# Fourth weight block of the gate/up pairs: residue 64 of 256 bytes in every second pair

## The chip, the core and the metric

The kernel runs on one core of a Trainium2 chip. Its engines work side by side and wait for each other through semaphores: TensorE (PE in the profile, with its weight loads shown apart as PEld), VectorE (DVE), ScalarE (ACT), GpSimd (POOL) and SyncE (SP, which here only issues DMAs). The on-chip memory has 128 partitions; an address below is a byte offset within a partition, the same in all 128. A *residue* is such an address modulo 256. The metric is the device time of one execution in microseconds; a run of a kernel is summed up by the median of its executions.

## The reference

One decoder layer, batch 1, 512 positions, width 1024, all in float32: three token mixers (a gated MLP, a sparse attention and a linear recurrence) side by side, their gated sum through an output projection, and then the feed-forward part, in which the change lies:

```python
hf = rms_norm(x, g_pre_ffn)
f_gate, f_up = jnp.split(hf @ w_ffn_in, 2, axis=-1)
f = (jax.nn.silu(f_gate) * f_up) @ w_ffn_out
return x + rms_norm(f, g_post_ffn)
```

`w_ffn_in` has 2 x 2816 columns: 22 blocks of 128 gate columns and 22 of 128 up columns.

## The kernel before

Every float32 product is made of three products in the type float32r: each operand is split into a high part (ScalarE copies it with rounding, line 125) and a low part (VectorE subtracts, line 130), and TensorE adds high x high, high x low and low x high. Of a matmul's two operands one is *stationary*: 128 x 128, loaded into the array by a weight load of its own. The other is *moving*: 128 partitions by 256 or 512 columns, streamed through. The weight load of one matmul goes on while the matmul ahead of it runs.

The program runs through its stages in one fixed order, written out in the calls at the end of `hybrid_block`: normalisation and the first projections, the recurrent mixer, the gated MLP, the attention, the three gated branches, the output projection (`wo_pass`, line 1059), the gate/up products of the feed-forward part, and its output product (`down`). The order of the work on each engine is that in which the code records it; buffers come from pools in which each tag has a fixed number of buffers, taken in turn.

**The gate/up pairs.** Each of the 22 pairs j is one gate block and one up block. The first two (`HEAD = 2`) are plain products (`ffn_head`). The other 20 are made by `pairs` (line 1315) with Strassen's scheme in Winograd's form: the weights of a pair are cut into four blocks a11, a12, a21, a22 of 128 x 512, the activations in the same way, and seven products replace eight. `pair_prep(j)` (line 1272) makes the weight side of the seven, in steps that are interleaved with the products of pair j - 1: raw weights come by DMA to a tile `rawp`; sums of blocks are formed on VectorE; each block and sum is split into a high and a low tile. The split blocks lie in a ring of five pairs of tiles (`hi`/`lo` and `u`), apart from the block a22, which has two tiles of its own (line 1295): `a22h` (tag "tg") and `a22l` (tag "q32"), each with two buffers, so that pairs alternate between them.

`product_parts(ps, j, a, b)` (line 1306) runs one of the seven products: four steps k, and in each three matmuls (high weights x high activations, high x low, low x high), 12 in all, with a weight slice of 128 x 128 as the stationary operand and an activation tile of 256 columns as the moving one. The product with a22 is called in `last(j)` (line 1321), after the second product of the next pair, and takes the activation side number 4.

**Where the operands lie.** The function `row` hands out tiles of 512 floats from the pool "mid", in three tags. Before the change every tile of the three tags has residue 0, as do the ring's tiles. The activation sides (tiles `t`, and `fh`/`fl`) are allocated with a first element of `MOVED = 16` floats, so they lie at residue 64. The slices of a weight tile are 512 bytes apart and those of an activation tile 1024 bytes, so the residue is the same for all four k.

**The other users of the two tags.** "tg" holds the gates of the branches (`gate_part`, line 1015, 24 tiles in all), "q32" the queries for the compressed attention (`q_tile`, line 733, 8 tiles; they are stationary operands at line 795), and `down` takes two tiles of each for partial sums (line 1437).

For comparison the prediction also uses `v_pair` (line 762), which runs matmuls of 256 columns with stationary slices of `hh`/`hl` and moving slices of weights, all at residue 0: in steps of 128 floats for the stationary operand over c, and 24 matmuls for each c.

Of the kernel before, what the change touches and what calls it, by code (L numbers as in the profile page):

```python
# [23 lines left out]
F32 = mybir.dt.float32  # L24
F32R = mybir.dt.float32r
# [5 lines left out]
S = 512  # L31
# [20 lines left out]
def hybrid_block(ctx: ExitStack, tc: tile.TileContext, A, out):  # L52
# [5 lines left out]
    mid = ctx.enter_context(tc.tile_pool(name="mid", bufs=1))  # L58
# [35 lines left out]
    def nm(s):  # L94
        cnt[0] += 1
        return f"{s}_{cnt[0]}"
# [6 lines left out]
        return t if len(shape) == 1 else t.rearrange(  # L103
            "p (a b) -> p a b" if len(shape) == 2 else "p (a b c) -> p a b c", **dict(zip("abc", shape)))

    def row(name, dt=F32, tag="row"):
        return mid.tile([128, S], dt, tag=tag, name=nm(name), bufs={"row": 6, "q32": 2, "tg": 2}[tag])

    def bank(tag):
        return psum[1].tile([128, S], F32, tag=tag, name=nm(tag), bufs=psum[2][tag])  # L110
# [13 lines left out]
    def split(src, hi, lo, lo_eng=None):  # L124
        res["hi"] = SC.activation(hi, src, AF.Copy)  # L125
        e = lo_eng or V
        if e is GP:
            GP.tensor_sub(lo, src, f32(hi))
        else:
            res["lo"] = V.tensor_sub(lo, src, f32(hi))  # L130
# [41 lines left out]
    HEAD, LASTV = 2, 2  # L172
# [186 lines left out]

    rmul = const.tile([128, 3, 4], F32, name="rmul")  # L360
    rbs = row("rbs")
    half = const0([128, 3, 8], "half")

    def norm():

        for i in range(2):
            for c in range(2):
                SC.activation(xr[i][:, c, :], xr[i][:, c, :], AF.Square, accum_out=ssx[:, 2 * i + c:2 * i + c + 1])
            q = slice(2 * i, 2 * i + 2)
            rsqrt(rstd[:, q], ssx[:, q], 2, 1.0 / D, EPS)  # L370
            V.tensor_scalar(rmul[:, 0, q], rstd[:, q], GELU_K ** 0.5, None, op0=OP.mult)
            V.tensor_scalar(rmul[:, 1, q], rstd[:, q], GELU_C, None, op0=OP.mult)
            V.tensor_mul(rmul[:, 2, q], rstd[:, q], rstd[:, q])
            yield
        few = softplus()
        for _ in range(19):
            next(few, None)
            yield
        rb = bank("tr")
        with tc.issue_after(res["mm"].ins):  # L380
            spread(rb, rstd)
        SC.activation(rbs, rb, AF.Copy)
        yield
        for k in range(NK):
            t = row("h32")
            V.scalar_tensor_tensor(t, xt[k], vec[:, V_PRE + k:V_PRE + k + 1], rbs, op0=OP.mult, op1=OP.mult)
            split(t, hh[k], hl[k])
            yield
        V.tensor_scalar(half[:, 0], vec[:, V_BX:V_BX + 8], 0.5, None, op0=OP.mult)
        V.tensor_scalar(half[:, 1], vec[:, V_LNG:V_LNG + 8], 0.5, None, op0=OP.mult)  # L390
        V.tensor_scalar(half[:, 2], vec[:, V_LNB:V_LNB + 8], 0.5, None, op0=OP.mult)
# [31 lines left out]
    def gelu2(x, dst, c=None):  # L423


        s = row("gs")
        SC.activation(s, x, AF.Square, scale=GELU_K ** 0.5 if c is None else rmul[:, 0, c:c + 1])
        V.scalar_tensor_tensor(s, s, 1.0, x, op0=OP.add, op1=OP.mult)
        SC.activation(s, s, AF.Tanh, scale=GELU_C if c is None else rmul[:, 1, c:c + 1])
        V.scalar_tensor_tensor(dst, s, 1.0, x, op0=OP.add, op1=OP.mult)  # L430
# [780 lines left out]
    def first_weights():  # L1211

        ff["raw"] = [slab("rawp", tag="w2", shape=(2, 1024))]
        pair_load(HEAD)
        for _ in range(9):
            yield
        w = [tuple(wts.tile([128, 1024], F32R, tag=t, name=nm(t), bufs=3) for t in ("hi", "lo")) for _ in range(3)]
        ff["ring"] = w
        ff["prep"] = pair_prep(HEAD)
        for _ in range(4):  # L1220
            next(ff["prep"])
            yield
# [45 lines left out]
    def pair_load(j):  # L1268
        if HEAD <= j < NFF:
            SY.dma_start(ff["raw"][(j - HEAD) % 2], A["w_fi"][2 * j:2 * j + 2].rearrange("u p n -> p u n"))  # L1270

    def pair_prep(j):

        if j >= NFF:
            return
        raw = ff["raw"][(j - HEAD) % 2]
        r4 = raw.rearrange("p u (h n) -> p (u h) n", h=2)
        a11, a12, a21, a22 = (r4[:, i] for i in range(4))
        g = [ff["ring"][(3 * (j - HEAD) + i) % 5] for i in range(3)]
        w = wa[j] = {}  # L1280

        def halves(u, *names):
            for i, n in enumerate(names):
                w[n] = tuple(t[:, 512 * i:512 * i + 512] for t in u)

        split(raw[:, 0], *g[0])
        halves(g[0], "a11", "a12")
        s13 = stage.tile([128, 1024], F32, tag="raw", name=nm("s13"), bufs=2)
        V.tensor_tensor(s13.rearrange("p (i n) -> p i n", i=2), r4[:, 0:4:3], a21[:, None, :].to_broadcast([128, 2, 512]),
                        op=OP.subtract)  # L1290
        yield
        split(s13, *g[1])
        halves(g[1], "s3", "s1")
        yield
        w["a22"] = row("a22h", F32R, "tg"), row("a22l", F32R, "q32")
        split(a22, *w["a22"])
        V.tensor_add(a21, s13[:, 512:], a11)
        yield
        V.tensor_sub(a22, a12, a21)
        yield  # L1300
        split(raw[:, 1], *g[2])
        halves(g[2], "s2", "s4")
        pair_load(j + 2)
        yield
# [10 lines left out]
    def pairs():  # L1315
# [11 lines left out]

        for j in range(HEAD, NFF):
            prep = pair_prep(j + 1)
            z, y = ff["zy"] if j == HEAD else (bank("mm")[:, :256], bank("mm"))  # L1330
            r1, r3 = row("r1"), row("r3")
# [405 lines left out]
```

## Time and profile before

| | |
|---|---|
| median of three runs | 1112.24 us |
| the three runs | 1112.24, 1109.35, 1112.64 us |
| the profiled execution | 1111.33 us |
| its span, first to last instruction | 1109.6 us |
| granted TensorE clock, mean | 0.998 |
| instructions in the span | 15969 |

A row of a group in the profile reads: line, engine, operation, output <- inputs, partitions x elements, count | busy time in us, mean duration of one in ns | idle time of the engine just ahead, and what ended it. An answer for one line or one tile has count, then the shortest, median and longest duration in ns, then the first and last start. A row of stretches reads: start and end in us, length, and then for each engine the busy time and in brackets the count of the instructions that overlap the stretch, and last the granted clock, the share of the DMA engines and GB/s. Where the row is for one line, it has the columns of TensorE and of its weight loads alone. A row of the timeline reads: start, duration, engine, line, operation, and in square brackets the idle time ahead of it and what ended it. Matmuls overlap: the next one starts while the one ahead still drains, so a duration is a latency, and the distance from start to start is the pace.

### The profile page before, as it was taken

How to read it: one execution, taken by the hardware profiler on the slowest of the kernel's cores; microseconds unless marked ns; L12 is line 12 of the kernel's file. 1: busy time of each engine (PE TensorE's matmuls, PEld its weight loads, DVE VectorE, ACT ScalarE, POOL GpSimd, SP SyncE). 2: the span in 40 equal slices, each digit the busy share in tenths (PEclk: the TensorE clock that was granted, in tenths of full speed). 3: DMA queues.
4: the chain of work that ended last, by engine and by line, in shares of the span. 5: the costliest groups of instructions: out<-in, count | busy, mean ns of one | idle time of the engine just before them, and what ended most of it. 6: DMA issues, size and time to landing. Idle time of an engine off the chain costs nothing.

```text
span 1109.6 us, 15969 instructions
## 1 busy us (share of the span) xinstructions
PE 1100.5 (99%) x6152; PEld 951.7 (86%) x6152; DVE 827.9 (75%) x1453; ACT 626.1 (56%) x1120; POOL 46.4 (4%) x59
## 2 busy tenths in 40 slices
PE   9999999999999999999999999999999999999997
PEld 8888778888888887888888888888999999998886
DVE  6966968263575899998998844557988888879665
ACT  6756674232344676876776733435655655567552
POOL 1000203000000000000000000000000000022200
PEclk9999999999999999999999999999999999999999
DMA  8332325323222211102112163331233322378902
GB/s 311 114 95 76 98 94 192 112 82 106 81 91 77 76 58 38 58 20 77 58 39 67 48 241 101 114 115 38 77 115 115 107 104 95 133 192 216 186 33 95
DMA packets 34652, 115.02 MB, mean 104 GB/s; under 512 B 3408, under 2 KB 3696, under 8 KB 33424
## 3 DMA queue, kind: packets, MB, share of 16 engines
q1 hardware_dynamic: 27200, 93.78, 25.4%
q0 software_dynamic: 5216, 11.18, 5.0%
q10 hardware_dynamic: 2160, 9.04, 2.3%
q8 instruction: 48, 0.79, 0.3%
q14 instruction: 28, 0.23, 0.1%
HBM read 111.89 MB, written 2.10 MB: 103 GB/s over the span
## 4 chain that ended last, share of the span: by engine, by line
PE 93%; DVE 4%; ACT 1%; DMA 0%; issue 0%; DVEq 0%
PE mm L242 39%; PE mm L1310 18%; PE mm L1446 7%; PE mm L545 4%; PE mm L1074 4%; PE o L895 4%; PE sc L857 3%; PE tr L882 3%; PE tr L1446 3%; PE mm L773 2%; PE tr L689 1%; PE mm L1176 1%; DVE lo L130 1%; PE tr L470 1%; PE tr L605 1%; PE tr L795 1%
## 5 line engine op out<-in xcount | busy, mean ns | idle before, releaser
L125 ACT ACTIVATE hi<-raw 128x1024 fp32r<-128x1024 f32 (+1 forms) x108 | 113.4, 1050 | 155.4 <-PE mm L242 81.2
L242 PE MATMUL mm<-hh,hi 128*128 128x512 f32 x504 | 199.7, 396 | 0.0
L242 PE MATMUL mm<-hh,lo 128*128 128x512 f32 x504 | 197.5, 392 | 0.2 <-DVE lo L130 0.2
L242 PE MATMUL mm<-hl,hi 128*128 128x512 f32 x504 | 197.1, 391 | 0.0
L130 DVE TENSOR_TENSOR lo<-raw,hi 128x1024 fp32r<-128x1024 f32 (+1 forms) x108 | 132.0, 1222 | 79.3 <-ACT hi L125 72.1
L242 PEld LDWEIGHTS mm<-hh,lo 128*128 128x128 f32 x504 | 94.6, 188 | 19.9 <-DVE lo L130 0.5
L242 PEld LDWEIGHTS mm<-hh,hi 128*128 128x128 f32 x504 | 94.8, 188 | 18.7 <-ACT hi L125 0.4
L242 PEld LDWEIGHTS mm<-hl,hi 128*128 128x128 f32 x504 | 94.7, 188 | 18.4 <-issue 0.2
L863 ACT ACTIVATE P<-P,ast 128x128 f32<-128x128 f32 (+3 forms) x128 | 70.7, 555 | 23.2 <-DVE ast L861 22.6
L861 DVE CUSTOM_DVE_ANT_0 P<-sc,mask 128x128 f32<-128x128 f32 (+3 forms) x128 | 57.9, 484 | 8.2 <-PE sc L857 7.3
L125 ACT ACTIVATE ph<-tr 128x512 fp32r<-128x512 f32 x80 | 47.0, 592 | 29.0 <-PE tr L882 28.1
L130 DVE TENSOR_TENSOR pl<-tr,ph 128x512 fp32r<-128x512 f32 x80 | 54.4, 685 | 4.9 <-ACT ph L125 2.7
L1310 PE MATMUL mm<-t,hi 128*128 128x256 f32 x288 | 52.4, 279 | 0.0
L1397 POOL DMA_DIRECT2D bs<-in_w_fo x16 | 19.3, 1213 | 788.5 <-DVE lo L130 788.5
L857 PE MATMUL sc<-K,q 128*128 128x512 f32 (+2 forms) x192 | 51.0, 368 | 0.0
L1446 PE MATMUL mm<-hi,u 128*128 128x512 f32 x160 | 50.4, 390 | 0.0
L882 PE MATMUL tr<-ident,P 128*128 128x128 f32 x320 | 48.7, 273 | 0.0
L882 PEld LDWEIGHTS tr<-ident,P 128*128 128x128 f32 x320 | 39.1, 140 | 9.7 <-DVE pl L130 1.0
L130 DVE TENSOR_TENSOR lo<-bs,hi 128x1024 fp32r<-128x1024 f32 x28 | 34.1, 1221 | 14.5 <-ACT hi L125 14.5
L1310 PEld LDWEIGHTS mm<-t,hi 128*128 128x128 f32 x288 | 44.0, 188 | 0.0
L1310 PE MATMUL mm<-fh,hi 128*128 128x256 f32 x144 | 40.4, 281 | 0.0
L1310 PE MATMUL mm<-t,lo 128*128 128x256 f32 x144 | 40.3, 280 | 0.0
(384 smaller groups left out, 2752.1 us busy)
## 6 DMA issues: line engine op xcount, KB each, us to landing
raw<-in_w_in SPq DMA_DIRECT2D x64, 512.0 KB, 3.5
rawp<-in_w_fi SPq DMA_DIRECT2D x20, 1024.0 KB, 4.9
raw<-in_w_br SPq DMA_DIRECT2D x24, 512.0 KB, 3.5
bs<-in_w_fo POOLq DMA_DIRECT2D x20, 512.0 KB, 8.0
w<-in_cw ACTq DMA_DIRECT2D x4, 1024.0 KB, 5.1
raw<-in_w_o SPq DMA_DIRECT2D x8, 512.0 KB, 3.5
bs<-in_w_fo SPq DMA_DIRECT2D x8, 512.0 KB, 7.8
raw<-in_w_v SPq DMA_DIRECT2D x7, 512.0 KB, 5.0
```

What stands on the lines that cost most here:

```text
L125: res["hi"] = SC.activation(hi, src, AF.Copy)
L130: res["lo"] = V.tensor_sub(lo, src, f32(hi))
L242: res["mm"] = PE.matmul(ps[:m, n0:n1], w[:, k * 128:k * 128 + m], x[k][:, n0:n1], start=(t == 0), stop=(t == 3 * NK - 1))
L545: res["mm"] = PE.matmul(b[c], x[k][:, c * 128:(c + 1) * 128], w[:, kk * 512:kk * 512 + 512], start=(k == 0 and t == 0), stop=(k == NK - 1 ...
L857: PE.matmul(ps[:, :w * n].rearrange("p (b n) -> p b n", b=w), lhs, K[:, i, brs[0]:brs[-1] + 1, :n], start=(i == 0), stop=(i == 1))
L861: V.tensor_tensor_reduce(out=t, in0=ps[:, b * n:b * n + n], in1=mask[0][:, S - n:], scale=-0.125, scalar=3.0e38, op0=OP.add, op1=OP.min, a ...
L863: SC.activation(t, t, AF.Exp, scale=-1.0, bias=st[:, 0, j, b:b + 1], accum_out=st[:, 1, j, b:b + 1])
L882: PE.transpose(pt[:, j * 128:(j + 1) * 128], self.part(j, br)[:, kt * 128:(kt + 1) * 128], ident)
L895: PE.matmul(po, VV[:, kt, g % 2, br].rearrange("p i d -> p (i d)"), x, start=(br == 0 and kt == 0 and t == 0), stop=(br == 1 and kt == a a ...
L1074: res["mm"] = PE.matmul(b[c, f], x[k][:, q], w[:, fs], start=(k == 0 and t == 0), stop=(k == NK - 1 and t == 2))
L1310: res["mm"] = PE.matmul(ps, w[:, k * 128:k * 128 + 128], x[:, k], start=(start and k == t == 0), stop=(k == 3 and t == 2), skip_group_chec ...
L1446: PE.matmul(ps, a, b, start=id(ps) not in begun, stop=i == len(ops) - 1, skip_group_check=True)
```

## The change

The tiles of the tags "tg" and "q32" become 32 floats longer, 544 instead of 512 (2176 bytes instead of 2048), and `row` gets an argument that says at which of these floats the 512 in use begin. Only the two tiles of a22 use it, with 16 for the pairs 2, 4, 6, ... and 32 for the pairs 3, 5, 7, ...:

```diff
-    def row(name, dt=F32, tag="row"):
-        return mid.tile([128, S], dt, tag=tag, name=nm(name), bufs={"row": 6, "q32": 2, "tg": 2}[tag])
+    def row(name, dt=F32, tag="row", first=0):
+        bufs = {"row": 6, "q32": 2, "tg": 2}[tag]
+        return mid.tile([128, S if tag == "row" else S + 32], dt, tag=tag, name=nm(name), bufs=bufs)[:, first:first + S]
...
-        w["a22"] = row("a22h", F32R, "tg"), row("a22l", F32R, "q32")
+        side = (16, 32)[(j - HEAD) % 2]
+        w["a22"] = row("a22h", F32R, "tg", side), row("a22l", F32R, "q32", side)
```

In the built program the buffers lie as follows (bytes; the a22 column is where the tile in use begins):

| buffer | before | after, buffer | after, a22 | residue of a22 |
|---|---|---|---|---|
| tg, first | 29952 | 29952 | 30016 | 64 |
| tg, second | 32000 | 32128 | 32256 | 0 |
| q32, first | 34048 | 34304 | 34368 | 64 |
| q32, second | 36096 | 36480 | 36608 | 0 |

Gates, queries and the partial sums of `down` begin at the start of their buffers, that is at residue 0 in the first and 128 in the second. The six tiles of the tag "row" keep their addresses. All pools behind "mid" (raw weights, ring, activations and the rest) lie 512 bytes further on, so their residues stay. The instructions of all engines are the same, in the same order, with the same waits.

## The prediction

> **What bounds the kernel now.** I read the profile page first, for the engine that sets the end, then the busy time by stage, then how fast matmuls follow each other in the stage that the change touches.
>
> ```profile
> span 1109.6 us, 15969 instructions
> PE 1100.5 (99%) x6152; PEld 951.7 (86%) x6152; DVE 827.9 (75%) x1453; ACT 626.1 (56%) x1120; POOL 46.4 (4%) x59
> PEclk9999999999999999999999999999999999999999
> PE 93%; DVE 4%; ACT 1%; DMA 0%; issue 0%; DVEq 0%
> PE mm L242 39%; PE mm L1310 18%; PE mm L1446 7%; PE mm L545 4%; PE mm L1074 4%; PE o L895 4%; PE sc L857 3%; PE tr L882 3%; PE tr L1446 3%; PE mm L773 2%; PE tr L689 1%; PE mm L1176 1%; DVE lo L130 1%; PE tr L470 1%; PE tr L605 1%; PE tr L795 1%
> ```
>
> TensorE is busy for 99% of the span, the clock is granted in full in every slice, and the chain that ended last runs through TensorE for 93% of it. The gate/up pairs are line 1310, 18% of the chain. So an edit counts only if it makes TensorE wait, or changes how fast one matmul follows the next.
>
> ```profile
> 793.00:1007.00 214.00, 214.00 (x1760) 211.27 (x1759) 179.11 (x225) 129.96 (x221) 7.89 (x8) 1.00 0.38 126
> L1310 PEld LDWEIGHTS mm<-t,a22h x160: 187/188/188, 806.2 to 995.6; 128*128 128x128 f32 x160
> L1310 PE MATMUL mm<-t,a22h x160: 279/279/282, 806.3 to 995.7; 128*128 128x256 f32 x160
> L1310 PE MATMUL mm<-t,a22l x80: 279/280/283, 806.6 to 995.8; 128*128 128x256 f32 x80
> ```
>
> The first row is the pair stage from 793 to 1007 us: after the stretch's length come the busy times of PE, PEld, DVE, ACT and POOL with their counts, then the granted clock (1.00), the DMA share and GB/s. TensorE has no idle time there, while VectorE has 35 us and ScalarE 84 us. The other rows are the matmuls that read the changed tiles: 160 with a22h and 80 with a22l as the stationary operand, 240 in 20 pairs, 12 a pair. None of them waits for an operand. The 279 ns is the latency of one; what costs span is the pace, the time from one start to the next.
>
> **What the change does.** It adds, removes and reorders no instruction, on any engine, and no buffer gets a new wait: both tags keep two buffers. What differs is addresses. A buffer of 2176 bytes is 8.5 times 256, so the second buffer of each tag begins 128 bytes off the first. Pairs 2, 4, 6 ... (j minus HEAD even) start 16 floats in, in the first buffer: residue 64. Pairs 3, 5, 7 ... start 32 floats in, in the second: 128 + 128 = 256, residue 0. The tags' earlier uses number 24 (gates) and 8 (queries), both even, so the first pair does get the first buffer. The moving operand of the a22 product, tile t, is allocated with MOVED = 16, at residue 64 for all pairs. So today the weights lie 64 bytes off the moving operand. Afterwards 10 of the 20 pairs have both at 64, that is at the same residue, and 10 are as before. The edit touches 10 x 12 = 120 of the program's matmuls.
>
> **The price of equal residues.** The trace has both relations at 256 columns. Below are three stretches, each with TensorE busy throughout: the pairs (line 1310, weights at 0, moving at 64), the first v_pair (line 773, weights and moving both at 0), and the output projection (line 1074, 512 columns, both at 0).
>
> ```profile
> 810.00:960.00 150.00, 150.00 (x1276) 150.00 (x1275) 1.00 0.30 107
> 350.30:361.30 11.00, 11.00 (x94) 11.00 (x94) 1.00 0.17 48
> 735.00:755.00 20.00, 20.00 (x90) 16.57 (x89) 1.00 0.22 77
> ```
>
> A count includes the records that began ahead of the left edge and still run: a latency divided by a pace, 2.4 records at 256 columns and 1.7 at 512. So the paces are 150 / (1276 - 2.4) = **117.8 ns** for the pairs, 11 / (94 - 2.4) = **120.1 ns** for line 773, and 20 / (90 - 1.7) = 226.5 ns for 512 columns. The last two differ by 106.4 ns for 256 more columns, so 0.416 ns is a column and a fixed part remains: 120.1 - 106.4 = 13.7 ns with equal residues, 117.8 - 106.4 = 11.4 ns with weights 64 bytes off. Equal residues cost 2.3 ns a matmul. Single operations of the two groups say the same:
>
> ```profile
> L1310 PEld LDWEIGHTS mm<-t,hi 128*128 128x128 f32 x288 | 44.0, 188 | 0.0
> L773 PEld LDWEIGHTS mm<-hi,hh 128*128 128x128 f32 x32 | 6.1, 192 | 0.0
> L773 PE MATMUL mm<-hi,hh 128*128 128x256 f32 x32 | 9.1, 283 | 0.0
> L242 PEld LDWEIGHTS mm<-hh,hi 128*128 128x128 f32 x504 | 94.8, 188 | 18.7 <-ACT hi L125 0.4 <-issue 0.2
> ```
>
> At 256 columns a weight load takes 192 ns with equal residues and 188 ns with a difference of 64 bytes; a matmul 283 against 279 ns. (The last row, 512 columns with both operands at 0, comes back below.) I read this as the next matmul's weight load meeting the running matmul's reads. Line 773 differs in more than the residue (other tiles, another stride of the moving operand), so this is a likeness, not a proof.
>
> The term is therefore 120 x 2.3 ns = **+0.28 us**. A loss on TensorE in this stage goes to the end undiminished, since nothing there hides it.
>
> Bounds. Below: no pace can go under the columns themselves, so the most to gain is the fixed part, 120 x 11.4 ns = -1.4 us. Above, the nearest row is the 2.3 ns; as an outer end I allow as much again as the whole fixed part, +1.4 us. I take +0.28, the value of the row that has the relation itself.
>
> **The splits that write the tiles.** ScalarE and VectorE now write, and VectorE reads, at residue 64 in half the pairs.
>
> ```profile
> 807.84 0.63 ACT L125 ACTIVATE a22h<-rawp 128x512 fp32r<-128x512 f32 x1 [0.91 <-PE mm L1310]
> 808.50 0.69 DVE L130 TENSOR_TENSOR a22l<-rawp,a22h 128x512 fp32r<-128x512 f32 x1 [1.00 <-ACT a22h L125]
> 826.13 0.40 PE L1310 MATMUL mm<-t,a22h 128*128 128x256 f32 x2
> ```
>
> ScalarE waits 0.91 us for the matmuls that still read the buffer, then writes it; VectorE is done at 808.50 + 0.69 = 809.19 us. The buffer serves two products later: a pair has 84 matmuls, 84 x 117.8 ns = 9.9 us, and the product that uses it starts at 826.13 us. That leaves 16.9 us. Doubling both splits would take 1.3 us of it. I cost it at nothing; if the slack were gone it would be at most 10 x 1.3 = 13 us, which no size of 64 bytes explains.
>
> **Everything else that moves.** The pools behind "mid" move by 512 bytes. Within line 773 the stationary slices step by 128 floats, 512 bytes, and one pace holds through the whole 11 us stretch, so a shift by 512 bytes changes no relation that the pace reacts to. The second buffers of gates and queries now lie at residue 128. Gates are read by VectorE alone; queries are weights in line 795:
>
> ```profile
> L795 PEld LDWEIGHTS tr<-kcb,q x64: 187/192/192, 361.5 to 551.1; 128*128 128x128 f32 x64
> L795 PE MATMUL tr<-kcb,q x64: 217/275/275, 361.6 to 551.2; 128*128 128x64 f32 x64
> L1020 ACT ACTIVATE tg<-mm 128x512 f32<-128x512 f32 x24 | 14.0, 583 | 2.4 <-PE mm L242 2.4
> ```
>
> Half of 64 records, at a few ns either way, is within 0.2 us; the 24 gate writes wait for TensorE and not the reverse. I cost both at nothing.
>
> **The sum.** The profiled execution took 1111.33 us (span 1109.6 us). 1111.33 + 0.28 = **1111.6 us**. That execution is 0.9 us under the median of the three runs, 1112.24 us, and inside their spread of 1109.35 to 1112.64; against the median the same sum gives 1112.5 us. About 0.3%, 3.3 us, is what a measurement of this kernel can tell from no change, so the term itself will not show in the times, only in the trace.
>
> **Rivals.**
> - *The residue of the weights does not matter*, and line 773 is slower for its own access pattern. For it: 512-column matmuls have equal residues too, and their loads take the same 188 ns. Against it: there the load covers only half of the matmul, 16.57 of 20.00 us, so a meeting can be avoided. It gives +0.00, 1111.3 us. The Trainium skill bears on this ("TensorE: Matmul & The Clock Gate", section "Step-by-step: what each phase is for"): TensorE has two independent SBUF read ports, and loading the next weights does not steal read bandwidth from the running matmul. By that rule the result would be this rival's; the 120.1 against 117.8 ns speaks against it, but not finally. The same page's "Back-to-back issue gap" has N / 2.4 + 2.5 ns, an estimate of 109.2 ns for 256 columns; both rows are above it.
> - *The new place is better*: what helps is a residue other than 0 on the weights, whatever the moving operand has. No row has weights at 64. It gives at most the fixed part, -1.4 us, 1109.9 us.
> - *Slower, beyond the noise*: at equal residues in this loop the load would no longer lie beneath the running matmul. Then the pace of the 120 goes from 117.8 to the load's 188 ns, +70 ns each: +8.4 us, 1119.7 us. It would decide from 3.3 us / 120 = 28 ns a matmul on. Against it stands line 773, where loads at equal residues lie beneath matmuls the whole time, at 120 ns.
> - *The change does not do what it says*: with the two buffers exchanged, the residues would be 128 and 192. The even counts above exclude it.
>
> **How the numbers follow.** The forecast, slower by 0.28 us: 0.68. No effect: 0.19. The new place is better: 0.10. The load uncovered: 0.03. Only the last leaves the band of 0.3%; run-to-run spread can put a measured difference out of it on either side, for which I allow 0.02 each, taken from the first three. So faster 0.02, same 0.93, slower 0.05. The range runs from the lowest run shown less the bound of gain, 1109.35 - 1.4 = 1108.0, to the highest plus the outer loss, 1112.64 + 1.4 = 1114.0.
>
> **What would show it.** Right: in the pair stage the a22 products alternate, 12 matmuls in about 1.44 us (120 ns) and in 1.41 us (117.8 ns); the weight loads of a22h have two values, 188 and 192 ns; all other groups of line 1310 stay at 279 to 280 ns; the stage is 0.3 us longer; ScalarE's and VectorE's splits stay near 0.63 and 0.69 us. Wrong: one pace for all a22 products (no effect), one below 117 ns (better), idle time of TensorE ahead of an a22 load or a pace near 188 ns (uncovered), or a changed pace in a group that is not a22, which would mean that the shift by 512 bytes or the gates and queries count after all.

## The result, and the profile after

| | before | after |
|---|---|---|
| median | 1112.44 us (4 runs: 1112.24, 1109.35, 1112.64, 1112.67) | 1105.36 us (4 runs: 1106.26, 1104.46, 1105.33, 1105.39) |
| profiled execution | 1111.33 us | 1106.26 us |
| its span | 1109.6 us | 1104.6 us |
| ratio after / before | | 0.9943, 95% interval 0.9923 to 0.9962 |

The change makes the kernel faster by 0.57%, about 7 us between the medians and 5.1 us between the two profiled executions. The prediction had 1111.6 us within 1108.0 to 1114.0; the time lies under that range. The page of after, with the span, the busy times, the clock, and the chain that ended last by engine and by line (lines of code are one or two further down than before: 1310 is now 1312):

```profile
span 1104.6 us, 15969 instructions
PE 1095.1 (99%) x6152; PEld 946.0 (86%) x6152; DVE 828.2 (75%) x1453; ACT 625.2 (57%) x1120; POOL 46.5 (4%) x59
PEclk9999999999999999999999999999999999999999
PE 95%; DVE 2%; ACT 1%; DMA 0%; issue 0%; DVEq 0%; ACTq 0%
PE mm L243 43%; PE mm L1312 17%; PE mm L1448 6%; PE mm L546 4%; PE mm L1075 4%; PE o L896 4%; PE sc L858 3%; PE tr L883 3%; PE tr L1448 3%; PE mm L774 2%; PE tr L690 1%; PE mm L1177 1%; PE tr L471 1%; DVE lo L131 1%; PE tr L606 1%; PE tr L796 1%
```

The instructions and their counts are those of before, the clock is full in both, and TensorE is still busy for 99%. It has simply been busy for less: 1095.1 against 1100.5 us. No wait was removed; the same matmuls follow each other faster. The rows of stretches say where. First the whole pair stage on all engines, then two stretches of line 1312 alone:

```profile
793.00:1007.00 214.00, 213.90 (x1784) 210.15 (x1783) 183.45 (x231) 132.66 (x226) 7.89 (x8) 1.00 0.40 131
808.00:826.00 18.00, 18.00 (x155) 18.00 (x154) 1.00 0.33 117
828.00:845.00 17.00, 17.00 (x152) 17.00 (x152) 1.00 0.20 70
```

In the same 214 us TensorE now overlaps 1784 matmuls, where it had 1760. By the prediction's way of counting, the pace is 18 / (155 - 2.4) = 118.0 ns up to 826 us, which is the 117.8 ns of before, and 17 / (152 - 2.4) = 113.6 ns from 828 us on. A count is a whole number, so a pace from it is good to one record in the count: 0.1 ns over 150 us, 0.8 ns over 17 us, 2 ns over 7 us. From start to start in the records the two stretches have 117.8 and 113.3 ns, and these two values come back in every stretch below that is called long or short. Most matmuls in both stretches are ones whose residues the edit leaves alone. The rows of the changed tiles:

```profile
L1312 PEld LDWEIGHTS mm<-t,a22h x160: 186/188/192, 806.2 to 990.3; 128*128 128x128 f32 x160
L1312 PE MATMUL mm<-t,a22h x160: 276/280/373, 806.3 to 990.4; 128*128 128x256 f32 x160
L126 ACT ACTIVATE a22h<-rawp x20: 616/632/636, 723.1 to 971.1; 128x512 fp32r<-128x512 f32 x20
L131 DVE TENSOR_TENSOR a22l<-rawp,a22h x20: 684/689/696, 724.4 to 971.8; 128x512 fp32r<-128x512 f32 x20
```

The loads of a22h reach up to 192 ns and the matmuls now go from 276 ns, where every one had 279 to 282. The splits are as they were, at 0.63 and 0.69 us. The timeline of TensorE (start, duration, operation) shows the turn, at the first matmuls of six products; a product is 12 matmuls, so its length is the distance to the next one's start:

```profile
804.93 1.58 PE L1312 MATMUL mm<-t,u 128*128 128x256 f32 x12
806.34 0.40 PE L1312 MATMUL mm<-t,a22h 128*128 128x256 f32 x2
807.78 0.40 PE L1312 MATMUL mm<-t,hi 128*128 128x256 f32 x2
...
826.15 0.40 PE L1312 MATMUL mm<-t,a22h 128*128 128x256 f32 x2
827.58 0.39 PE L1312 MATMUL mm<-t,hi 128*128 128x256 f32 x2
828.94 0.28 PE L1312 MATMUL mm<-fh,u 128*128 128x256 f32 x1
```

Up to 806 us a product takes 806.34 - 804.93 = 1.41 us, as before. The first a22 product with its weights at residue 64 takes 1.44 us, just as predicted, and 1.41 us follows again. The second one (pair 4, 826.15) takes 1.43 us, but the product behind it, with both operands at the residues that they always had, takes 828.94 - 827.58 = 1.36 us, and this goes on to the end of the stage, at 986 us, apart from shifted products and one wait.

So the stage has **two paces for the same matmuls**: a *long* one, 1.4135 us a product (117.8 ns a matmul), and a *short* one, 1.360 us (113.3 ns). Measured from start to start in the records, after has 108 products at the short pace: 108 x 53.5 ns = 5.8 us less. Seven a22 products at 1.440 us give back 0.19, those of pairs 2 and 4 0.05, and one with a wait at 845 us 0.11. The net is 5.4 us; the stage ends 5.25 us earlier (990.65 against 995.90 us) and the span is 5.0 us shorter. The profile of before is at the long pace in all 138 products from 798 us on.

### The profile page after: what moved, and what is told of

Read it like the earlier page. It is cut to its first block, busy times and chain, and to the rows that moved or that the text cites. A ratio compares the mean times of both kernels' runs of the same rounds, so it can differ in the third digit from the quotient of the medians.

```text
span 1104.6 us, 15969 instructions
## 1 busy us (share of the span) xinstructions
PE 1095.1 (99%) x6152; PEld 946.0 (86%) x6152; DVE 828.2 (75%) x1453; ACT 625.2 (57%) x1120; POOL 46.5 (4%) x59
## 4 chain that ended last, share of the span: by engine, by line
PE 95%; DVE 2%; ACT 1%; DMA 0%; issue 0%; DVEq 0%; ACTq 0%
PE mm L243 43%; PE mm L1312 17%; PE mm L1448 6%; PE mm L546 4%; PE mm L1075 4%; PE o L896 4%; PE sc L858 3%; PE tr L883 3%; PE tr L1448 3%; PE mm L774 2%; PE tr L690 1%; PE mm L1177 1%; PE tr L471 1%; DVE lo L131 1%; PE tr L606 1%; PE tr L796 1%
```

## The experiments

What had to be settled: whether the shifted weights bring about the short pace, or something else that the edit moves (the padding, the 512 bytes, residue 128 of gates and queries), or chance, since one run of before had 1109.35 us. Behind each time stands the ratio to the kernel before, measured beside it on the same chip, with its 95% interval. Diffs marked "side" are against the changed kernel, the others against the one before.

**The padding alone.** The tiles stay longer, so everything that the edit moves is moved, but the weights of a22 are at residue 0 in all pairs.

```diff
-        side = (16, 32)[(j - HEAD) % 2]
+        side = (0, 32)[(j - HEAD) % 2]
```

> The longer tiles, the shift by 512 bytes and the residue of 128 for gates and queries as in the change, but a22 at residue 0 in all pairs. Theory A (the equal-residue products at 64 push the distance between weight loads and matmuls out of a slow steady pace of 117.8 ns into a fast one of 113.3 ns, which then holds by itself): all pairs at 117.8 ns, no switch, about 1112 us, 0.3% or less from before. Rival B (the layout around a22 brings the gain): 113.3 ns and about 1105 us.

Measured: 1110.95 us, 10 executions, 1110.13 to 1113.07; ratio 1.001 (0.9994 to 1.0025). The gain is gone. Its profile holds a surprise, though, in two stretches of line 1312:

```profile
798.00:815.00 17.00, 17.00 (x153) 17.00 (x152) 1.00 0.23 68
820.00:970.00 150.00, 150.00 (x1276) 150.00 (x1275) 1.00 0.32 110
```

It entered the stage at the short pace, 17 / (153 - 2.4) = 112.9 ns, for 13 products, met a wait of some 0.08 us at 815.3 us, in an a22 product, and was at 117.8 ns from there to the end (124 products). So the short pace can be there without shifted weights; and what was lost at the wait did not come back.

**Shifted weights in two pairs, and in one.** Residue 64 only in pairs 2 and 4, then only in pair 4.

```diff
-        side = (16, 32)[(j - HEAD) % 2]
+        side = (16 if j <= HEAD + 2 else 0, 32)[(j - HEAD) % 2]      # two pairs
+        side = (16 if j == HEAD + 2 else 0, 32)[(j - HEAD) % 2]      # one pair
```

> Residue 64 for a22 in pairs 2 and 4 alone, 0 in the others. In the changed kernel the pace went to 113.3 ns in the a22 product of pair 4. Theory A: the same history up to there, then 113.3 ns to the end of the stage without a further push, and 8 products that cost 1.36 us in place of 1.44 us: about 0.6 us under the changed kernel, 1104.7 us. Rival C (the fast pace needs a push in every second pair): back to 117.8 ns some products after pair 4, about 1111 us.

> Residue 64 for a22 in pair 4 alone. Theory A: if one product of 12 is enough to switch, 117.8 ns before 826 us and 113.3 ns after, about 1104.7 us; but pair 2's push did not switch in the changed kernel, so the outcome may hang on where in its cycle of three matmuls the product begins, and 117.8 ns throughout (1112 us) is as well possible; no pace between the two for long. Rival C: a gain for a few products at most, about 1112 us.

Measured: two pairs 1109.4 us (0.9988, 0.9969 to 1.0007), with single executions spread from 1104.44 to 1112.34; one pair 1110.97 us (1.0004, 0.9986 to 1.0022), with one of ten at 1104.64. The profile of two pairs is of an execution of 1106.3 us:

```profile
799.00:805.00 6.00, 6.00 (x56) 6.00 (x55) 1.00 0.00 0
830.00:930.00 100.00, 100.00 (x885) 100.00 (x884) 1.00 0.31 108
945.00:980.00 35.00, 35.00 (x299) 35.00 (x299) 1.00 0.36 124
```

It was at the short pace on entry, passed both shifted products without leaving it (100 / (885 - 2.4) = 113.3 ns), met a wait at 939.6 us and had the long pace afterwards, 35 / (299 - 2.4) = 118.0 ns. In the profile of one pair the long pace held from end to end; the shifted product at 825.7 us did not end it. So a shifted product does not always end the long pace. And the short one held without further shifted products from 826 to 938 us, over 11 a22 products with their weights at 0, so it needs no push in every second pair (rival C); but it was lost at the wait and did not come back. The median, 1109.4 us, lies between the two forecasts, 1104.7 and 1111 us.

**The two kernels again.** The kernel before with one execution and a profile, and the changed kernel twice, on other chips.

> The kernel before, once more, for a second trace of it. Theory A: the pair stage is again at 117.8 ns from 797 us to its end, with 113.3 ns nowhere or, if the pace can switch by chance, from some point on; about 1112 us, or down to 1107 us with a switch by chance.

> The changed kernel itself, for more executions. Theory A (two steady paces; a wait can drop TensorE from the fast to the slow one, and a product with equal residues can lift it back): every execution is lifted back within a few pairs, so all lie between about 1104 and 1108 us, none near 1111; the trace has 113.3 ns for most of the stage, whatever pace it enters with. Rival D (the four fast executions were luck, as two of 25 executions of the kernel before took 1105.7 and 1106.1 us): a mixture with many near 1111 us.

> The changed kernel beside the two below on the same chip. Theory A: all executions within 1104 to 1108 us, 0.5% to 0.6% under the kernel before, whose executions are mostly near 1111 us.

Measured: before 1111.73 us, long pace in all 138 products; after 1105.86 us (0.9942, 0.9926 to 0.9959) and 1106.14 us (0.9956, 0.9944 to 0.9969). The gain repeats. All 13 executions of the changed kernel lie between 1104.46 and 1108.05 us. Of all 113 of the kernel before, 106 lie between 1109.03 and 1114.62, and 7, found on four of the chips, between 1103.61 and 1106.91, with none in the gap. Those 7 were not profiled; executions of the short pace, without a shifted product, are the reading that fits their times. It also fits that the pace on entry varies: of the 16 profiles in which the first products of the stage have their operands 64 bytes apart, 6 enter at the short pace, the padding alone among them.

**Shifted weights in every pair.** The two buffers of each tag get lengths that put a22 at residue 64 in all pairs.

```diff
-        return mid.tile([128, S if tag == "row" else S + 32], dt, tag=tag, name=nm(name), bufs=bufs)[:, first:first + S]
+        return mid.tile([128, S + {"row": 0, "tg": 16, "q32": 48}[tag]], dt, tag=tag, name=nm(name), bufs=bufs)[:, first:first + S]
...
-        side = (16, 32)[(j - HEAD) % 2]
-        w["a22"] = row("a22h", F32R, "tg", side), row("a22l", F32R, "q32", side)
+        side = ((16, 48), (0, 0))[(j - HEAD) % 2]
+        w["a22"] = row("a22h", F32R, "tg", side[0]), row("a22l", F32R, "q32", side[1])
```

> a22 at residue 64 in all 20 pairs (tiles longer by 16 and 48 floats, so that both buffers can lie at 64). Theory A: a push in every pair, so a drop lasts one or two pairs at most; but 10 more products of 1.44 in place of 1.36 us: +0.8 us. About 1105 to 1106.5 us, all executions close together. If equal residues only cost and the alternation matters: no switch, 117.8 ns, and 20 x 27 ns more than before, about 1112 us.

> a22 at residue 64 in all pairs, as e6. If moving the weights is what pushes: about 1106 to 1107 us again, 113.3 ns in most of the stage. If e6 and e15 differed by their chips: like e18, both fast or both slow.

Measured: 1106.94 us (0.9952, 0.9937 to 0.9967), and on another chip 1106.47 us (0.9973, 0.9956 to 0.999). Their intervals overlap those of the change. The short pace began behind the shifted product at 806 us in one profile, and at 816 us, behind the second, in the other.

**All pairs at equal residues; 128 and 192 bytes apart.** The moving tiles are allocated elsewhere, for all products of the stage; the weights stay at 0.

```diff
-    MOVED = 16
+    MOVED = 0        # and 32, and 48
```

> The kernel before with MOVED = 0: moving and stationary operands at residue 0 in all of the pairs and of the two plain ones. The prediction's term (equal residues make 120 ns): one pace, 120 ns, in all 1680 products' matmuls and no second one, 2.2 ns x 1680 = +3.7 us, about 1115 us. If line 773 was slow for another reason: 113 to 118 ns, 1106 to 1112 us.

> The kernel before with MOVED = 32: the moving operands of the pairs 128 bytes off the weights instead of 64. If the paces hang on the distance in bytes: one or two steady paces other than 117.8 and 113.3 ns, between 107 and 120. If only equal or unequal matters: 117.8 and 113.3 ns by chance as before, about 1111 us.

> The kernel before with MOVED = 48: moving operands at 192, weights at 0, 192 bytes apart (or 64 on the other side of 256). If the pace hangs on the distance alone, whatever its sign: 117.8 or 113.3 ns by chance, 1106 to 1112 us. Else another steady pace, between 107 and 120 ns: 1094 to 1115 us.

Measured: residue 0 1115.7 us (1.0033, 1.0021 to 1.0045), 128 1115.2 us (1.0026, 1.0016 to 1.0035), 192 1111.08 us (1.0011, 0.9994 to 1.0027). A stretch of line 1310 for each, in this order:

```profile
810.00:960.00 150.00, 150.00 (x1253) 150.00 (x1252) 1.00 0.31 107
```

```profile
830.00:930.00 100.00, 100.00 (x845) 100.00 (x844) 1.00 0.31 106
```

```profile
830.00:930.00 100.00, 100.00 (x851) 100.00 (x850) 1.00 0.30 106
```

The paces are 150 / (1253 - 2.4) = 119.9 ns (120.0 from start to start), 100 / (845 - 2.4) = 118.7 and 100 / (851 - 2.4) = 117.8. Equal residues cost what the prediction said: 20 pairs x 84 matmuls x 2.3 ns = 3.9 us, and the time is 3.9 us over the 1111.8 us of before, measured beside it. None of the three profiles had a short pace. At 128 the profile is of an execution of 1113.31 us; six of the ten took 1115.18 to 1115.98 us, about 2 us more, and none of them was profiled.

**a22 at residue 128 instead.** If the relation "both at 64" did it, another place of the weights would not. First in every second pair, then in all.

```diff
-        side = (16, 32)[(j - HEAD) % 2]
+        side = 32                          # 128 in every second pair, 0 in the others
+        side = (32, 0)[(j - HEAD) % 2]     # 128 in all pairs
```

> As the changed kernel, but a22 of every second pair at residue 128 instead of 64: 64 bytes off the moving operand on the other side. Theory A in its narrow form (a push needs a product with equal residues): no push, so executions that enter slow stay at 117.8 ns, about 1111 us. In its wide form (any product with another pace moves the weight loads against the matmuls): lifted as in the changed kernel, about 1105.5 us. The a22 products at 128 also show the pace at that side.

> a22 at residue 128 in every second pair, 0 in the others. Theory A in its wide form: lifted like the changed kernel, and its a22 products cost 1.36 in place of 1.44 us in the fast pace, up to 10 x 0.08 = 0.8 us under e12. Narrow form (equal residues push better): some executions stay slow for longer, 0.5 us or more over e12.

> a22 at residue 128 in all pairs. Wide form of theory A: a push in every pair and no product at 120 ns, so the fast pace is reached within two or three pairs and found again after each wait: the fastest of the three, about 0.8 to 1.2 us under e12. Narrow form: like e13 or slower.

Measured: every second pair 1106.08 us (0.9969, 0.9954 to 0.9984) and, on another chip, 1107.14 us (0.9965, 0.9952 to 0.9979); all pairs 1105.74 us (0.995, 0.9937 to 0.9962). The first row is the first kernel's, of line 1312 behind the turn, which came at its second shifted product, 826 us; the second row is its a22 group:

```profile
850.00:980.00 130.00, 130.00 (x1150) 130.00 (x1149) 1.00 0.35 118
```

```profile
L1312 PE MATMUL mm<-t,a22h x160: 276/276/385, 806.2 to 989.6; 128*128 128x256 f32 x160
```

The pace is 130 / (1150 - 2.4) = 113.3 ns, and the a22 products take part in it (median 276 ns, against 280 in the changed kernel). So neither equal residues nor the residue 64 of the weights is needed to end the long pace: 128, on the other side of the moving tile, does it too, and without the 1.44 us. Against the changed kernel measured beside them (1106.14 us), all pairs at 128 is 0.4 us lower, where the wide form had 0.8 to 1.2, and every second pair at 128 is 1.0 us higher, which is the side of the narrow form; the intervals separate neither. In that run's profile the short pace was lost at a wait at 940 us, in a product at 128, and came back two pairs later.

**The moving tile of the a22 product instead.** The weights stay at 0; only the activation side number 4 moves, to residue 0 (equal to the weights) or 192. This has the relations of the runs above, with the other operand shifted.

```diff
-        t = {n: slab("t", F32R, "mo", (2, 4, 256), MOVED) for n in (1, 2, 3, 4)}
+        t = {n: slab("t", F32R, "mo", (2, 4, 256), 0 if n == 4 else MOVED) for n in (1, 2, 3, 4)}     # residue 0
+        t = {n: slab("t", F32R, "mo", (2, 4, 256), 48 if n == 4 else MOVED) for n in (1, 2, 3, 4)}    # residue 192
```

> The kernel before, with the activation tile of the a22 product alone at residue 0 instead of 64; a22 stays at 0, nothing else moves. Theory A (the relation of the two operands): as with a22 at 64 in all pairs: 120 ns in the a22 products, 113.3 ns in most of the rest, about 1106 to 1107 us. Rival B (the tiles of a22 or the layout): 120 ns in 240 matmuls and 117.8 ns in the rest, 0.5 us over the kernel before.

> The kernel before, with that activation tile at residue 192, 64 bytes on the other side of the weights at 0. Theory A, wide form: as with a22 at 128 in all pairs: 113.3 ns in most of the stage, the a22 products included, about 1105 to 1106 us. Rival B: 117.8 ns throughout, as before.

> The moving tile of the a22 product at residue 0, weights at 0, as e15. If moving the weights is what pushes: slow again, 1111 to 1112 us, with 117.8 ns outside the a22 products. If the chips made the difference: like e17.

Measured: residue 0 1111.87 us (1.0001, 0.9992 to 1.0011), and on another chip 1111.66 us (1.0016, 0.9997 to 1.0036); residue 192 1111.43 us (0.9996, 0.9987 to 1.0006). No gain: the 20 executions at residue 0 all took 1110.93 us or more. The second profile at residue 0, stretches of line 1310:

```profile
798.00:805.00 7.00, 7.00 (x64) 7.00 (x63) 1.00 0.00 0
820.00:930.00 110.00, 110.00 (x933) 110.00 (x932) 1.00 0.32 106
```

This execution entered at the short pace (7 / (64 - 2.4) = 113.6 ns); its first a22 product, at 805.6 us, took 1.44 us with no wait, and the products behind it were back at the long pace, for good: 110 / (933 - 2.4) = 118.2 ns is one product in seven at 120 ns and six at 117.8. The theory that any product with another relation between its operands ends the long pace falls here. What remains is narrower: **the place of a22's weights has to change, not the moving tile's**; a change of the moving tile to residue 0 was here followed by the opposite.

**The weight ring at 64.** The tiles `hi`/`lo` of the pool "wts" at residue 64, and the moving ones at 128, so that the products with `hi`/`lo` keep their 64 bytes and the 512-column matmuls of line 242 get them too. The two ring tiles `u` come from the pool "big", behind both pads (64 + 192 = 256 bytes), and so stay at residue 0, as a22 does: these products have their operands 128 bytes apart.

```diff
+    wts.tile([128, 16], F32, name="side0", bufs=1)
...
+    big.tile([128, 48], F32, name="side1", bufs=1)
...
-    MOVED = 16
+    MOVED = 32
```

> The kernel before with the weight ring moved to residue 64 (a pad of 16 floats ahead of it, 48 behind) and MOVED = 32. In the 512-column stages weights and moving operands, now both at 0 (226.7 ns, 13.3 ns over their 512 columns), lie 64 bytes apart. If their 13.3 ns are the same meeting as the 13.3 ns of 120 ns: 220 to 224 ns there, 3 to 7 ns less on some 2600 matmuls, 8 to 18 us less. If a weight load of 188 ns in 227 ns avoids the meeting already: 226.7 ns as before. The pairs have unequal residues (64 and 128 apart) and may take 113 to 119 ns.

Measured: 1123.14 us (1.0123, 1.0091 to 1.0154), the slowest kernel of all. Line 242 in the profile of before, and the same line (now 244) here, between 260 and 280 us:

```profile
260.00:280.00 20.00, 20.00 (x90) 16.58 (x89) 1.00 0.31 101
```

```profile
260.00:280.00 20.00, 20.00 (x87) 16.13 (x86) 1.00 0.29 81
360.00:367.00 7.00, 7.00 (x62) 7.00 (x61) 1.00 0.17 66
```

With 512 columns the pace went from 20 / (90 - 1.7) = 226.5 to 20 / (87 - 1.7) = 234.5 ns, or from 226.7 to 233.3 ns from start to start: there equal residues are the better place, at least against weights 64 bytes further on than the moving operand. The last row is line 773 (now 775), whose operands were at equal residues and are now 64 bytes apart: 7 / (62 - 2.4) = 117.4 ns instead of 120.1, or 117.8 instead of 120.0 from start to start. That is what the prediction lacked: nothing but the address of the moving operand differs there, so the extra 2.2 ns come from the residues, not from the tiles or strides. In the pairs, products with `hi` take 1.413 us on average (64 bytes apart), those with `u` and a22 1.425 to 1.428 (128 apart, 118.7 to 119.0 ns). The weights' place changes from product to product here, between 64 and 0, and still no product took 1.360 us; so what shifted weights do was shown for a22 among weights at 0 and moving tiles at 64, and not in general.

**What the short pace meets.** In the second run of the changed kernel the timeline of three engines around 940 us reads (in brackets the idle time ahead and what ended it):

```profile
934.35 1.23 DVE L1290 TENSOR_TENSOR s<-rawp 128x1024 f32<-128x1024 f32 x1 [4.01 <-DMA rawp<-in_w_fi]
...
938.08 1.06 ACT L126 ACTIVATE hi<-rawp 128x1024 fp32r<-128x1024 f32 x1 [5.12 <-DVE rawp L1301]
...
940.51 0.36 ACT L1370 ACTIVATE r<-mm 128x256 f32<-128x256 f32 x1
...
940.93 0.50 PE L1312 MATMUL mm<-t,a22h 128*128 128x256 f32 x2 [1.59 <-ACT r L1370]
```

The same sum in the profile of before:

```profile
936.84 1.23 DVE L1289 TENSOR_TENSOR s<-rawp 128x1024 f32<-128x1024 f32 x1 [1.52 <-DMA rawp<-in_w_fi]
```

From 850 us on, every second of these loads is waited for by 1.5 to 1.8 us in both kernels, and this one by 4.01 us. So ScalarE's split is late, behind it its copy of the product's result (line 1370), and TensorE waits 1.59 us; from the start of the product ahead to that of the waiting one are 3.11 us instead of 1.36, so this costs 1.75 us. Six of the eight profiles of kernels with shifted weights throughout have a wait at this place, which costs 0.15 to 1.75 us ahead of the a22 product. In this trace the a22 product behind the wait has shifted weights, and the short pace goes on; in those of the padding alone and of two pairs it had them at residue 0, and the long pace followed.

## Why the prediction was wrong

- **The price of equal residues: right.** The forecast was 12 matmuls in about 1.44 us; the a22 products at residue 64 take 1.440 to 1.443 us wherever no turn and no wait falls into them. The run with equal residues in all pairs gave the predicted 2.3 ns a matmul (+3.9 us for all of them), and the ring run showed line 773 to be slow for the same reason. From start to start the price is 2.2 ns; the prediction's 2.3 came from counts, of which that of 11 us is good to 1.3 ns only.
- **"The edit touches 120 matmuls" and 117.8 ns as the pace of the rest: the step that failed.** The sum priced only the 120 whose residues change, and took the pace of the other 1560 of the stage as given; the bound below, -1.4 us, was worked out from the 120 alone. The runs showed that 117.8 ns is one of two paces that these matmuls hold by themselves, and that products with shifted weights can bring them into the other. The gain is 108 products x 53.5 ns = 5.8 us on matmuls whose residues the edit leaves alone. One row could have made me ask: the runs of before differed by 3.3 us (1109.35 to 1112.64), which I put down to measurement. With TensorE busy for 99% at a full clock, a difference of pace is one thing that can lie behind such a spread; whether it did in that execution is not known, as it was not profiled.
- **Splits, the shift by 512 bytes, gates and queries at 128: rightly priced at nothing.** The padding alone has the shift, the gates and the queries and gives 1.001 (0.9994 to 1.0025); the splits kept their 0.63 and 0.69 us.
- **Undiminished to the end: right.** The net of 5.4 us within the stage became 5.0 us of span. The splits' slack held; but in some executions a late load of raw weights, which the prediction did not look at, takes some of the gain back.
- **Rivals.** "The residue does not matter" is refuted by the run with all products at residue 0. The Trainium skill says under "TensorE: Matmul & The Clock Gate", section "Step-by-step: what each phase is for", that loading the next weights steals no read bandwidth from the running matmul, through two independent ports; here the same 1680 matmuls took 120.0, 118.7 or 117.8 ns with nothing but the addresses of the moving tiles changed, so the measurement decides against it as a rule for the time. "The new place is better" was the nearest by sign, but not by mechanism: at residue 64 the a22 products themselves are slower, and at its bound it explains 1.4 us of 5. "Load uncovered" did not occur.
- **What would show it.** The last clause, "a changed pace in a group that is not a22", is what happened. Its reading there, that the 512 bytes or the gates count after all, is not: the padding alone had no gain.

How far the cause is settled: over all profiles, of the shifted a22 products that TensorE came to at the long pace and that had no wait in them, 8 of 12 were followed by the short one (4 of 7 at residue 64, 4 of 5 at 128). With a22's operands as before there were 19 such products with another one behind them in before, 19 in its second profile and 18 in that of one pair, and none was followed by it. The times agree: every kernel that shifts a22's weights throughout is faster, none that leaves them is.

A second count says what the waits do. Those that TensorE met at the short pace all fell on an a22 product (first start to second over 170 ns, near 815, 824, 845, 940 and 961 us). The short pace went on behind nine of nine with the weights at residue 64, three of five at 128 and none of three at 0. So a wait by itself does not end the short pace; what follows it goes with the place of the weights. Shifted weights thus stand at both kinds of place: where the long pace ends, and where the short one outlasts a wait.

What the runs leave open: why shifted weights do it and a shifted moving tile does not; why a shifted product sometimes fails to; and what decides at which pace an execution enters the stage.

## What to carry to other kernels

When an engine is busy all the time and still differs by some tenths of a per cent between executions, look for two paces of the same instructions before a price is put on an edit: list start-to-start distances over the stage, in more than one profile. A pace read from one trace is a state, not a constant, and an edit of a few instructions can move the state for all that follow; its bound is then the whole stage, here 1680 x 4.5 ns = 7.6 us, not the edited part. And a residue that helps at 256 columns can hurt at 512, so each shape is to be measured by itself.

## What the runs showed of the hardware

- The stage runs at 117.8 or 113.3 ns a matmul with the same instructions, addresses and full clock, and each pace holds for over a hundred products. In the records the two differ in where the next weight load begins: on average 2.5 ns after the running matmul's start at the long pace and 3.3 ns at the short one, in all profiles with the ring at 0 and the moving tiles at 64. That is a mark by which to tell them there; with the moving tiles at 192 the long pace has 3.3 ns too, and whether the offset has a part in the cause was not tried.
- The pace at 256 columns goes with how far the moving tile lies behind the weights, modulo 256 bytes: 120.0 ns at 0, 117.8 or 113.3 at 64, 118.7 at 128 (in the one execution profiled), 117.8 at 192, where the a22 products with weights at 128 also had 113.3. At 512 columns it is 226.7 ns at 0 and 233.3 at 192 (weights at 64, moving tile at 0).
- Shifting the stationary operand and shifting the moving one are not the same, even where the distance comes out equal: with both operands of the a22 products at equal residues, moving the weights gave 0.9942 to 0.9973, and moving the streamed tile 1.0001 and 1.0016.
